# A two-layer decoder trunk on one core: every second weight block split into its two parts by GpSimd's transfers instead of by ScalarE and VectorE

## The chip, the cores and the metric

The kernel runs on one core of a Trainium2 chip. The metric is the device time of one execution in microseconds, as the median of the runs of a kernel; smaller is better. Beside it stands one execution taken by the hardware profiler, whose first to last instruction is the span.

## What is computed

The reference is a decoder trunk of two layers over 256 tokens with a model width of 2048, all in float32:

```
for i in range(2):
    hn = rms_norm(h, norm_mix[i])
    h = h + (sb_gla_mixer(hn, ...) if i == 0 else ssd_mixer(hn, ...))
    h = h + squared_relu_mlp(rms_norm(h, norm_mlp[i]), mlp_w_up[i], mlp_w_down[i])
    h = h + sigmoid(h @ ple_w_gate[i]) * (p[i] @ ple_w_proj[i])
return rms_norm(h, final_norm)
```

The first mixer is stick-breaking attention beside gated linear attention, the second a state-space mixer with a short convolution. Nearly all of the arithmetic lies in the dense products: the input projections of the mixers (2048 to some 6144 and 10240 columns), their output projections, the MLP (2048 to 8192 and back, twice) and the gate (2048 to 2048, twice). What matters here is that the weights, some 500 MB, are each used once, and that every product is to have nearly float32 accuracy.

## The kernel before, in words

Activations are held feature-major: a tile has 128 features on the partitions and the 256 tokens along the row. Each activation operand is kept as two parts side by side, a rounded part "hi" in the type float32r in columns 0 to 255 and the remainder "lo" in columns 256 to 511 (split_into, line 103). Weights are split in the same way. A product is then hi x hi + hi x lo + lo x hi.

feature_major (line 112) does almost all dense products. It takes groups of output columns (width 4 means four tiles of 128 columns, so four PSUM banks of 512 columns); for each group it goes over kb_n blocks of the contraction. A block is 1 MB: four 128-row slices of weights with 512 columns each, laid out as 128 partitions x 2048 elements. For every block it

- loads it into a tile wraw with one DMA on SP's queue (load_block, line 94; the very first block in two halves),
- and for each half block (two slices, 128 x 1024 elements, 512 KB) calls split_weights (line 85): ScalarE copies wraw into whi, rounding it (line 88), and VectorE writes wlo = wraw - whi (line 89),
- then issues, for each of the four banks, two matmuls with whi as the stationary operand against all 512 columns of the activation (hi and lo, line 128) and two with wlo against the 256 columns of the activation's hi (line 133).

So a half block is sixteen matmuls. After the last block of a group, evac is called for each bank: ScalarE copies the bank's right half out of PSUM (line 168), VectorE adds it to the left half (line 169), and what follows depends on the stage (a scaling at line 171; an addition into the residual on GpSimd at lines 274, 300 and 339; a split of the result into the next operand at lines 106 to 110). token_major (line 143) does the same for the value projections with the activation as the stationary operand; it covers 16 blocks of 1 MB.

The tiles wraw, whi and wlo come from one pool with three buffers each (line 55). A buffer is given to a new tile when all readers of the old one are done: a whi buffer when TensorE has run the half block's matmuls, a wraw buffer when VectorE has made both remainders. The order of the instructions on each engine's queue is fixed before the run by the tile framework, which plans it with the program's order as priority and inserts all waits; at run time every queue is in order. Small side computations of the mixers are woven between blocks by pace (line 401).

SP's queue carries the weight loads, ScalarE's queue some small loads and eight broadcasts. GpSimd issues no transfers; it does elementwise work of 0.7 to 1.2 us each, mostly the additions into the residual.

Of the kernel before, what the change touches and what calls it, by code (L numbers as in the profile page):

```python
# [16 lines left out]
P = 128  # L17
# [8 lines left out]
def hybrid_trunk(  # L26
# [56 lines left out]
    rstd2 = keep.tile([P, T], F32, name="rstd2")  # L83

    def split_weights(dst, src_raw, cols):
        hi = wts.tile([P, cols], F32R, tag="whi", name="whi", padded_shape=[P, 1024])
        lo = wts.tile([P, cols], F32R, tag="wlo", name="wlo", padded_shape=[P, 1024])
        nc.scalar.copy(out=hi, in_=src_raw)  # L88
        nc.vector.tensor_tensor(out=lo, in0=src_raw, in1=hi.bitcast(F32), op=ALU.subtract)  # L89
        return hi, lo  # L90

    halve = [True]

    def load_block(src, cols=2048):
        raw = wts.tile([P, cols], F32, tag="wraw", name="wraw", padded_shape=[P, 2048])
        if halve.pop() if halve else False:
            nc.sync.dma_start(raw[:, : cols // 2], src[:, : cols // 2])
            nc.sync.dma_start(raw[:, cols // 2 :], src[:, cols // 2 :])
        else:
            nc.sync.dma_start(raw, src)  # L100
        return raw
# [8 lines left out]
            nc.vector.scalar_tensor_tensor(out=lo, in0=value, scalar=g, in1=hi.bitcast(F32), op0=ALU.mult, op1=ALU.subtract)  # L110

    def feature_major(blocks, kb_n, xt, evac, width=4, kts=4, evac_last=None):
        """blocks: DRAM access patterns, kb_n per group of `width` output tiles."""
        for grp, srcs in enumerate(blocks):
            banks = [acc_ps.tile([P, 512], F32, tag="acc", name=f"acc{n}") for n in range(width)]
            cols = kts * width * P
            per = 1024 // (width * P)
            if per > kts:
                per = kts
            for kb in range(kb_n):  # L120
                raw = load_block(srcs[kb], cols)
                for c0 in range(0, kts, per):
                    hi, lo = split_weights(None, raw[:, c0 * width * P : (c0 + per) * width * P], per * width * P)
                    for n in range(width):
                        for j in range(per):
                            k = kb * kts + c0 + j
                            o = (j * width + n) * P
                            nc.tensor.matmul(banks[n], lhsT=hi[:, o : o + P], rhs=xt(k),  # L128
                                             start=(k == 0), stop=False, skip_group_check=True)
                        for j in range(per):  # L130
                            k = kb * kts + c0 + j
                            o = (j * width + n) * P
                            nc.tensor.matmul(banks[n][:, T : 2 * T], lhsT=lo[:, o : o + P], rhs=xt(k)[:, 0:T],  # L133
                                             start=False, stop=(k == kb_n * kts - 1), skip_group_check=True)
                yield
            if evac_last is not None and grp == len(blocks) - 1:
                evac_last(banks)
            else:
                for n in range(width):
                    evac(grp * width + n, banks[n])  # L140
            yield

    def token_major(blocks, kb_n, xt, evac):
        """out[token, column] with the activations stationary."""
        for grp, srcs in enumerate(blocks):
            banks = [acc_ps.tile([P, 512], F32, tag="acc", name=f"acct{n}") for n in range(2)]
            for kb in range(kb_n):
# [23 lines left out]
            nc.vector.tensor_tensor(out=dst, in0=dst, in1=scale, op=ALU.mult)  # L171

    def gate_silu(dst, half):
        """dst = silu(2 * half)."""
        th = ev.tile([P, T], F32, tag="s", name="th")
        nc.scalar.activation(th, half, AF.Tanh)
        nc.vector.scalar_tensor_tensor(out=dst, in0=th, scalar=1.0, in1=half, op0=ALU.add, op1=ALU.mult)
# [7 lines left out]
            (eng or nc.gpsimd).tensor_tensor(out=sq_acc, in0=sq_acc, in1=sq, op=ALU.add)  # L185

    def newton(r, v):
        """r = 1/sqrt(v), one step: r * (1.5 - 0.5 v r^2)."""
        nc.vector.tensor_tensor(out=v, in0=v, in1=r, op=ALU.mult)
        nc.vector.scalar_tensor_tensor(out=v, in0=v, scalar=-0.5, in1=r, op0=ALU.mult, op1=ALU.mult)  # L190
        nc.vector.scalar_tensor_tensor(out=r, in0=v, scalar=1.5, in1=r, op0=ALU.add, op1=ALU.mult)

    def rstd_steps(mean=mean_d, squared=False, extra=(), in_psum=False):
        """rstd[:, t] = 1/sqrt(mean over features of the squares of token t + EPS), on every partition."""
        ms = small_ps(2, "ms")
        parts = [sq_acc, *extra]
        for i, sq in enumerate(parts):
# [65 lines left out]
            pass  # L263

    def out_stage(w, kb_n, xt, which, scale=None, before=None):
        """h += scale * (x @ w); returns the next stage's operand, gain applied, not yet normalized."""
        nxt = new_x()

        def evac(n, bank):
# [47 lines left out]
        return nxt, px  # L317

    def ple(i, x, px, mid):
        """h += sigmoid(x @ w_gate) * pp; returns h with the next norm's gain (split, but after the last layer)."""  # L320
        last = i == 1
        extra = []
        pp = [page([P, 8, T], f"pp{m}") for m in range(2)]
# [66 lines left out]
        yield  # L390

    def staggered(gens):
        """Step generator i of `gens` at ticks i, i + 1, ...; one tick per step, the youngest first."""
        live, gens = [], list(gens)
        while gens or live:
            if gens:
# [2 lines left out]
            yield  # L399

    def pace(main, sides):
        """Trace main; a side [after, every, generator] takes a step at step `after` of main and each `every` steps later.

        Sides may be added while main is traced, with `after` None for the next step."""
        n = 0
        for _ in main:
            n += 1
# [563 lines left out]
```

## Time and profile before

| | |
|---|---|
| median of 2 runs | 2781.89 us (2781.86 to 2781.91) |
| profiled execution, span | 2781.0 us |
| TensorE matmul busy | 2741.3 us (99%) |
| VectorE, ScalarE, GpSimd busy | 1848.8 (66%), 1440.0 (52%), 445.0 us (16%) |
| moved by DMA | 508.85 MB, mean 183 GB/s |
| granted TensorE clock, mean | 0.995 |

How to read the lines: a group of instructions has its source line, engine, operation, output and inputs, shape and count, then busy time and the mean duration of one in ns, and after the bar the idle time of its engine just before these instructions, with what ended it. PE is TensorE, PEld its loading of stationary weights, DVE is VectorE, ACT is ScalarE, POOL is GpSimd, SPq the queue of SP. A row of a timeline has the start in us, the length, the instruction, and in brackets the idle time before it. A row of stretches has its limits, its length, the busy time of each engine with the number of instructions, then the granted TensorE clock, the busy share of the DMA engines and GB/s. A row of issues has the count, the KB of each transfer and the median time from issue to landing in us.

### The profile page before, as it was taken

Reading aid. Unit: us, or ns where it says so; the run is one execution under the profiler, and the core shown is the slowest. Engines: PE = TensorE matmul, PEld = TensorE weight load, DVE = VectorE, ACT = ScalarE, POOL = GpSimd, SP = SyncE. Lnnn points to the kernel's source line nnn. Section 1 sums busy time; section 2 is a strip of 40 time slices with the busy share of each in tenths; the row PEclk is TensorE's granted clock in tenths of the full one; section 3 lists DMA queues with packets and bytes.
Section 4 is the critical chain, followed back from the end, with each engine's and each line's share of the span. In section 5 each row is a group of like instructions: output and inputs, shape, how many; then the busy total and the mean of one; then the engine's idle time right before and its main releaser. Section 6 shows DMA issues by size and latency. Waiting matters only on the chain.

```text
span 2781.0 us, 40169 instructions
## 1 busy us (share of the span) xinstructions
PE 2741.3 (99%) x15724; PEld 2371.0 (85%) x15724; DVE 1848.8 (66%) x2692; ACT 1440.0 (52%) x2180; POOL 445.0 (16%) x510
## 2 busy tenths in 40 slices
PE   7999999999999999999999999999999999999998
PEld 6888888888888888888888888888888888888887
DVE  7455676665666666679987888765666566666665
ACT  6455455544444444466555565554544444454455
POOL 4000031002002022133132122321100201102212
PEclk9999999999999999999999999999999999999998
DMA  5544355555555555554555555455555555555553
GB/s 208 187 167 152 125 180 195 184 195 184 195 184 195 187 191 187 178 186 155 212 197 177 183 186 190 172 184 185 194 182 188 191 189 189 188 195 186 193 175 129
DMA packets 72672, 508.85 MB, mean 183 GB/s; under 512 B 8656, under 2 KB 8848, under 8 KB 11936
## 3 DMA queue, kind: packets, MB, share of 16 engines
q1 hardware_dynamic: 70416, 497.58, 51.5%
q10 hardware_dynamic: 2064, 8.69, 0.9%
q8 instruction: 123, 2.02, 0.3%
q14 instruction: 69, 0.57, 0.1%
HBM read 504.07 MB, written 2.16 MB: 182 GB/s over the span
## 4 chain that ended last, share of the span: by engine, by line
PE 93%; DVE 4%; ACT 1%; POOL 1%; issue 1%; DMA 1%; DVEq 0%; ACTq 0%; POOLq 0%
PE acc L128 58%; PE acc L133 29%; DVE wlo L89 1%; PE acct L158 1%; PE acct L159 1%; PE acct L157 1%; DVE x L110 1%; PE y_ps L554 1%; ACT whi L88 1%; DVE yx L110 0%; PE y_ps L556 0%; POOL hn L239 0%; PE gla_o L836 0%; PE xs_tp L530 0%; PE st_ps L545 0%
## 5 line engine op out<-in xcount | busy, mean ns | idle before, releaser
L89 DVE TENSOR_TENSOR wlo<-wraw,whi 128x1024 fp32r<-128x1024 f32 x940 | 1179.4, 1257 | 826.2 <-ACT whi L88 824.3
L88 ACT CAST whi<-wraw 128x1024 fp32r<-128x1024 f32 x940 | 986.6, 1051 | 1051.7 <-PE acc L128 988.0
L128 PE MATMUL acc<-x,whi 128*128 128x512 f32 x4384 | 1386.4, 398 | 14.1 <-ACT whi L88 8.6
L133 PEld LDWEIGHTS acc<-x,wlo 128*128 128x128 f32 x4384 | 820.8, 189 | 200.3 <-DVE wlo L89 9.8
L133 PE MATMUL acc<-x,wlo 128*128 128x256 f32 x4384 | 863.2, 279 | 4.6 <-DVE wlo L89 4.6
L128 PEld LDWEIGHTS acc<-x,whi 128*128 128x128 f32 x4384 | 674.2, 190 | 22.5 <-ACT whi L88 8.6
L128 PE MATMUL acc<-hid,whi 128*128 128x512 f32 x2048 | 643.5, 395 | 0.0
L133 PEld LDWEIGHTS acc<-hid,wlo 128*128 128x128 f32 x2048 | 384.8, 188 | 90.9
L133 PE MATMUL acc<-hid,wlo 128*128 128x256 f32 x2048 | 403.0, 278 | 0.0
L300 POOL TENSOR_TENSOR h<-h,t_dn 128x256 f32<-128x256 f32 x128 | 152.9, 1205 | 1267.7 <-DVE t_dn L171 1266.9
L128 PEld LDWEIGHTS acc<-hid,whi 128*128 128x128 f32 x2048 | 311.8, 189 | 0.0
L168 ACT COPY right<-acc 128x256 f32<-128x256 f32 x422 | 153.2, 367 | 67.5 <-PE acc L133 66.5
L128 PE MATMUL acc<-yx,whi 128*128 128x512 f32 x512 | 161.4, 396 | 1.2 <-DVE sz L608 1.2
L133 PEld LDWEIGHTS acc<-yx,wlo 128*128 128x128 f32 x512 | 96.1, 188 | 23.3 <-DVE wlo L89 0.7
L185 POOL TENSOR_TENSOR sq_acc<-sq_acc,sq 128x256 f32<-128x256 f32 x98 | 96.7, 987 | 47.6 <-ACT sq L184 45.7
L133 PE MATMUL acc<-yx,wlo 128*128 128x256 f32 x512 | 100.9, 278 | 0.3 <-DVE wlo L89 0.3
L274 POOL TENSOR_TENSOR h<-h,t_out 128x256 f32<-128x256 f32 x32 | 37.6, 1193 | 291.8 <-DVE t_out L169 154.5
L128 PEld LDWEIGHTS acc<-yx,whi 128*128 128x128 f32 x512 | 78.1, 189 | 1.4 <-DVE sz L608 1.4
L171 DVE TENSOR_TENSOR t_dn<-t_dn,rstd 128x256 f32<-128x256 f32 x128 | 72.0, 583 | 0.8
L484 DVE SCALAR_TENSOR_TENSOR a_cv<-xp,cw,a_cv 128x256 f32<-128x256 f32 x144 | 65.7, 486 | 0.2
L110 DVE SCALAR_TENSOR_TENSOR x<-h,gain,x 128x256 fp32r<-128x256 f32 x64 | 47.5, 769 | 19.6 <-ACT x L109 19.6
L107 DVE TENSOR_TENSOR hid<-s_up,hid 128x256 fp32r<-128x256 f32 x128 | 50.7, 417 | 0.5 <-ACT hid L106 0.5
(245 smaller groups left out, 1790.0 us busy)
## 6 DMA issues: line engine op xcount, KB each, us to landing
wraw<-in_mlp_up_dram SPq DMA_DIRECT2D x128, 1024.0 KB, 4.9
wraw<-in_mlp_down_dram SPq DMA_DIRECT2D x128, 1024.0 KB, 4.9
wraw<-in_ssd_in_dram SPq DMA_DIRECT2D x80, 1024.0 KB, 4.9
wraw<-in_ab_in_dram SPq DMA_DIRECT2D x47, 1024.0 KB, 4.9
wraw<-in_ple_gate_dram SPq DMA_DIRECT2D x32, 1024.0 KB, 4.9
wraw<-in_ssd_out_dram SPq DMA_DIRECT2D x32, 1024.0 KB, 4.9
wraw<-in_ab_out_dram SPq DMA_DIRECT2D x16, 1024.0 KB, 4.9
rb<-acs_rows ACTq DMA_DIRECT2D x8, 1024.0 KB, 4.7
```

Of the source, the lines that this page charges most:

```text
L88: nc.scalar.copy(out=hi, in_=src_raw)
L89: nc.vector.tensor_tensor(out=lo, in0=src_raw, in1=hi.bitcast(F32), op=ALU.subtract)
L107: nc.vector.tensor_tensor(out=lo, in0=value, in1=hi.bitcast(F32), op=ALU.subtract)
L110: nc.vector.scalar_tensor_tensor(out=lo, in0=value, scalar=g, in1=hi.bitcast(F32), op0=ALU.mult, op1=ALU.subtract)
L128: nc.tensor.matmul(banks[n], lhsT=hi[:, o : o + P], rhs=xt(k), start=(k == 0), stop=False, skip_group_check=True)
L133: nc.tensor.matmul(banks[n][:, T : 2 * T], lhsT=lo[:, o : o + P], rhs=xt(k)[:, 0:T], start=False, stop=(k == kb_n * kts - 1), skip_group_c ...
L168: nc.scalar.copy(out=right[:rows], in_=bank[:rows, T : 2 * T])
L171: nc.vector.tensor_tensor(out=dst, in0=dst, in1=scale, op=ALU.mult)
L185: (eng or nc.gpsimd).tensor_tensor(out=sq_acc, in0=sq_acc, in1=sq, op=ALU.add)
L274: nc.gpsimd.tensor_tensor(out=h[:, n, :], in0=h[:, n, :], in1=t, op=ALU.add)
L300: nc.gpsimd.tensor_tensor(out=h[:, n, :], in0=h[:, n, :], in1=t, op=ALU.add)
L484: nc.vector.scalar_tensor_tensor(out=a, in0=xp[:, i : T + i], scalar=cw[:, blk, i : i + 1], in1=a, op0=ALU.mult, op1=ALU.add)
```

## The change

In feature_major, with width 4 and kts 4, every block with odd kb is no longer loaded into wraw. For each of its halves a new function dma_split takes a whi and a wlo tile and issues three instructions: a transfer on GpSimd's queue from the weights in DRAM into whi, which converts from float32 to float32r; on ScalarE wlo = -1 x whi; and a second transfer on GpSimd's queue of the same weights that is added to what stands in wlo. Even blocks, token_major and the narrow products keep the load on SP's queue and split_weights. The buffers change: whi and wlo have four each instead of three, wraw two instead of three (4 KB and 8 KB per partition each, so the sum stays the same). The diff, without the removed docstrings:

```
     def split_weights(dst, src_raw, cols):
-        hi = wts.tile([P, cols], F32R, tag="whi", name="whi", padded_shape=[P, 1024])
-        lo = wts.tile([P, cols], F32R, tag="wlo", name="wlo", padded_shape=[P, 1024])
+        hi = wts.tile([P, cols], F32R, tag="whi", name="whi", padded_shape=[P, 1024], bufs=4)
+        lo = wts.tile([P, cols], F32R, tag="wlo", name="wlo", padded_shape=[P, 1024], bufs=4)
         nc.scalar.copy(out=hi, in_=src_raw)
         nc.vector.tensor_tensor(out=lo, in0=src_raw, in1=hi.bitcast(F32), op=ALU.subtract)
         return hi, lo
 
+    def dma_split(src, cols):
+
+        hi = wts.tile([P, cols], F32R, tag="whi", name="whi", padded_shape=[P, 1024], bufs=4)
+        lo = wts.tile([P, cols], F32R, tag="wlo", name="wlo", padded_shape=[P, 1024], bufs=4)
+        nc.gpsimd.dma_start(hi, src)
+        nc.scalar.mul(lo, hi.bitcast(F32), -1.0)
+        nc.gpsimd.dma_start(lo, src, accum_op=ALU.add)
+        return hi, lo
...
     def load_block(src, cols=2048):
-        raw = wts.tile([P, cols], F32, tag="wraw", name="wraw", padded_shape=[P, 2048])
+        raw = wts.tile([P, cols], F32, tag="wraw", name="wraw", padded_shape=[P, 2048], bufs=2)
...
             for kb in range(kb_n):
-                raw = load_block(srcs[kb], cols)
+                by_dma = width == 4 and kts == 4 and kb % 2 == 1
+                raw = None if by_dma else load_block(srcs[kb], cols)
                 for c0 in range(0, kts, per):
-                    hi, lo = split_weights(None, raw[:, c0 * width * P : (c0 + per) * width * P], per * width * P)
+                    cs = slice(c0 * width * P, (c0 + per) * width * P)
+                    if by_dma:
+                        hi, lo = dma_split(srcs[kb][:, cs], per * width * P)
+                    else:
+                        hi, lo = split_weights(None, raw[:, cs], per * width * P)
```

## The prediction

> **What bounds the kernel now.** I read the head of the page first, then its groups, then the table of waits of each engine, then the timeline of ScalarE in a stretch where nothing special happens, because the change acts on a steady rhythm and its price has to be a price per beat.
>
> ```profile
> span 2781.0 us, 40169 instructions
> PE 2741.3 (99%) x15724; PEld 2371.0 (85%) x15724; DVE 1848.8 (66%) x2692; ACT 1440.0 (52%) x2180; POOL 445.0 (16%) x510
> q1 hardware_dynamic: 70416, 497.58, 51.5%
> L89 DVE TENSOR_TENSOR wlo<-wraw,whi 128x1024 fp32r<-128x1024 f32 x940 | 1179.4, 1257 | 826.2 <-ACT whi L88 824.3
> L88 ACT CAST whi<-wraw 128x1024 fp32r<-128x1024 f32 x940 | 986.6, 1051 | 1051.7 <-PE acc L128 988.0
> ...
> wraw<-in_mlp_up_dram SPq DMA_DIRECT2D x128, 1024.0 KB, 4.9
> ```
>
> TensorE is busy 99% of the span: only 2781.0 - 2741.3 = 39.7 us (1.4%) are left to gain. The two engines that the change relieves are not what it waits for. ScalarE idles 1051.7 us before its casts, 988.0 of them until TensorE has let go of a weight buffer, and VectorE idles behind ScalarE. So the splitting keeps up and waits for buffers. The loads wait too (the row of q1: 51.5% of 16 engines' time for 497.58 MB).
>
> The rhythm, from ScalarE's timeline:
>
> ```profile
> 880.62 1.05 ACT L88 CAST whi<-wraw 128x1024 fp32r<-128x1024 f32 x1 [1.47 <-PE acc L128]
> 883.41 1.05 ACT L88 CAST whi<-wraw 128x1024 fp32r<-128x1024 f32 x1 [1.73 <-PE acc L128]
> 886.19 1.05 ACT L88 CAST whi<-wraw 128x1024 fp32r<-128x1024 f32 x1 [1.74 <-PE acc L128]
> 888.98 1.05 ACT L88 CAST whi<-wraw 128x1024 fp32r<-128x1024 f32 x1 [1.73 <-PE acc L128]
> 891.77 1.05 ACT L88 CAST whi<-wraw 128x1024 fp32r<-128x1024 f32 x1 [1.73 <-PE acc L128]
> ```
>
> Four casts take 891.77 - 880.62 = 11.15 us, so TensorE eats one half block (512 KB of weights) in T = 2.79 us and one pair of blocks (even and odd, four halves) in 11.15 us. Each cast starts when a buffer comes free and takes 1.05 us: the present lead is comfortable, since the split of a half takes 1.05 + 1.26 = 2.3 us against the two halves (5.6 us) that TensorE still has in store with three buffers.
>
> **How often the change applies.** Blocks of 1 MB with width 4 and kts 4 in feature_major: 128 (mlp_up) + 128 (mlp_down) + 80 (ssd_in) + 32 (ab_in, 8 of its 12 column groups) + 32 (ple_gate) + 32 (ssd_out) + 16 (ab_out) = 448. Every second is 224, so 224 pairs of 11.15 us = 2498 us of the span run in the new rhythm.
>
> **What is removed.** Of 940 casts 448 become a negation of the same 128x1024 on ScalarE: I price it at the cast's 1.05 us, so no change there. 448 subtractions leave VectorE: 448 x 1.257 = 563 us of busy time. That gains nothing, since VectorE idled 824.3 us for ScalarE already. 224 loads leave SP's queue; SP then loads only even blocks into two buffers, each free a whole pair before it is needed: 11 us against the 4.9 us of a load. Hidden; if that cover went, it would cost the difference, which is negative.
>
> **What is added, and where it lies.** Each of the 448 odd halves now needs: a DMA on GpSimd's queue into hi (it waits until TensorE has released that hi buffer), a negation on ScalarE (waits for the landing), a second DMA on GpSimd's queue that adds the weights into lo (waits for the negation), then TensorE (waits for the landing). Nothing in this chain can begin before a buffer is free. With four buffers and four halves per pair, an odd half gets the buffer of the odd half one pair earlier, so between that release and its own use TensorE has three halves to work on: the cover is 3 x 2.79 = 8.36 us. What the chain takes beyond that is a TensorE stall, once per pair: the second odd half begins its chain one T later and is needed one T later, so it comes just in time behind the first. Should GpSimd's order be hi, lo, hi, lo rather than hi, hi, lo, lo, the stall moves ahead of the second half, while the pair's period stays chain + T as long as twice (hi + negation) does not exceed it.
>
> No transfer by GpSimd's queue, no converting and no accumulating one is in this trace, so both are bounded by the nearest rows.
>
> The nearest rows to GpSimd's handling of an instruction, to a wait on ScalarE, and to SP's handling of a load:
>
> ```profile
> L300 POOL TENSOR_TENSOR h<-h,t_dn 128x256 f32<-128x256 f32 x128 | 152.9, 1205 | 1267.7 <-DVE t_dn L171 1266.9
> L168 ACT COPY right<-acc 128x256 f32<-128x256 f32 x422 | 153.2, 367 | 67.5 <-PE acc L133 66.5
> ```
> ```profile
> 878.50 2.47 POOL L300 TENSOR_TENSOR h<-h,t_dn 128x256 f32<-128x256 f32 x2 [16.47 <-DVE t_dn L171]
> 881.40 0.74 POOL L300 TENSOR_TENSOR h<-h,t_dn 128x256 f32<-128x256 f32 x1 [0.43 <-DVE t_dn L171]
> 882.56 1.59 POOL L300 TENSOR_TENSOR h<-h,t_dn 128x256 f32<-128x256 f32 x1 [0.43 <-DVE t_dn L171]
> ```
>
> ```profile
> 5.91 0.33 SPq L100 DMA_DIRECT2D wraw<-in_ab_in_dram  x1
> ```
>
> And to the transfers:
>
> ```profile
> wraw<-in_ple_proj_dram SPq DMA_DIRECT2D x8, 512.0 KB, 3.5
> h<-in_xT_dram SPq DMA_DIRECT2D x4, 512.0 KB, 7.7
> ```
> ```profile
> 0.00:20.00 20.00, 11.05 (x44) 8.73 (x45) 9.97 (x14) 13.46 (x28) 10.50 (x33) 1.00 0.84 318
> ```
>
> A transfer of 512 KB lands 3.5 us after issue when it has the engines nearly to itself and 7.7 us in the opening, where the engines are busy to 0.84 at 318 GB/s. 512 KB more costs 4.9 - 3.5 = 1.4 us.
>
> The hi transfer: 3.5 us at best, 7.7 at worst. I take 3.5 + 0.7 + 0.7 = 4.9. The first 0.7 is GpSimd's own handling, taken as the shorter of its elementwise instructions (0.74 us at 881.40), against 0.33 us on SP. The second is half of the 1.4 us by which SP's next 1 MB load would slow it when both run together: that load is issued when the second even half has been split, just about when the odd buffer comes free.
>
> The negation: 1.05 us, plus 0.2 of waiting behind half an evacuation copy (the row of L168): 1.25 us. Zero to 1.05 us more if it meets an even half's cast; I keep 1.25.
>
> The accumulating transfer: it must read what stands in lo besides the weights. At best the reading of lo is free, 3.5; at worst 7.7. I take 3.5 + 0.7 + 1.4 = 5.6: one more stream of 512 KB through the same engines, and GpSimd's handling.
>
> A page of notes speaks against the change here: the Trainium skill, "Collectives: The Full Stack", section "The bandwidth ceiling: the fold count and why AG ≠ RS ≠ AR", says that a reducing transfer needs two source reads on the same ring and so moves at about half a copy's rate. No run here shows it yet; with the extra stream as priced above the sum is the forecast, and with a free read the chain would be 1.4 us shorter per pair.
>
> Chain: 4.9 + 1.25 + 5.6 = 11.75 us. Stall: 11.75 - 8.36 = 3.39 us per pair, 224 x 3.39 = 759 us.
>
> **The stall's echo in the clock.** This trace shows what a gap of such a length does (first the stretches, then TensorE's timeline):
>
> ```profile
> 64.00:66.00 2.00, 0.00 (x0) 0.00 (x0) 1.56 (x3) 2.00 (x6) 0.00 (x0) 1.00 0.00 0
> 66.00:68.00 2.00, 1.32 (x4) 1.14 (x5) 2.00 (x7) 1.08 (x2) 0.00 (x0) 0.52 0.35 53
> 68.00:70.00 2.00, 2.00 (x9) 1.72 (x9) 2.00 (x4) 0.00 (x0) 0.00 (x0) 0.62 0.93 381
> ```
> ```profile
> 66.68 1.22 PE L128 MATMUL acc<-x,whi 128*128 128x512 f32 x2 [3.15 <-DVE q L169]
> 67.70 0.63 PE L133 MATMUL acc<-x,wlo 128*128 128x256 f32 x2
> 68.13 1.06 PE L128 MATMUL acc<-x,whi 128*128 128x512 f32 x2
> 68.98 0.63 PE L133 MATMUL acc<-x,wlo 128*128 128x256 f32 x2
> 69.41 0.68 PE L128 MATMUL acc<-x,whi 128*128 128x512 f32 x2
> ```
>
> After 3.15 us without a matmul the granted clock is 0.52, and the eight matmuls from 66.68 to 69.41 take 2.73 us. At the rhythm of T for sixteen they would take 1.39: a loss of 1.34 us. A gap of 3.39 us stands at that edge, so I charge half of the pairs: 224 x 0.67 = 150 us (zero to 300).
>
> **GpSimd's old work.** Its queue is in order, and it often waits at its head for an evacuation (1266.9 us in the row of L300). Four adds per group hold GpSimd from 878.50 to 884.15. A transfer queued behind all four goes out up to 5.65 us late. This can hit one pair of each group: 32 groups of mlp_down, 4 of ab_out, 4 of ssd_out and 8 of ple_gate, 48 x 5.65 = 271 us at most. I take zero, because the first odd transfer of a group is ready one T before the group ends and stands ahead if the queue is ordered by readiness, and keep 271 for the upper end.
>
> **Sum.** 2781.0 + 759 + 150 = 3690 us; the medians shown lie 0.9 us above the span (2781.89), so about 3690 stands, some 33% slower. A change of 2% (56 us) is about what a measurement can tell from none.
>
> **Rivals.**
>
> (a) Hidden, the other side. If both transfers land in the time of the 3.5 us row, the chain is 3.5 + 1.05 + 3.5 = 8.05 us, under the cover of 8.36: TensorE never waits and the time is 2781, or down to 2781 - 40 if the relieved VectorE also closes the few gaps. It decides at a landing of (8.36 - 1.05) / 2 = 3.65 us per transfer. For it: the row of 3.5. Against: that row is of a quiet stretch and another queue, and these transfers meet each other and SP's loads. The Trainium skill, "DMA: Bandwidth & Descriptors", section "Anatomy of one DMA — SWDGE (gpsimd) path", gives about 2.0 us plus bytes over 436e9 for a GpSimd transfer; by it 512 KB would take an estimated 3.2 us, and it is this rival. Chance 0.06 (0.01 of it faster by over 2%).
>
> (b) The engines' throughput decides, not latency. By q1's row 1.0486 MB costs 0.515 x 2781 x 1.0486 / 497.58 = 3.02 us of all 16 engines. A pair now takes 6.03 us of 11.15; with a plain load, a converting and an accumulating block at one and two streams 3.02 + 3.02 + 6.03 = 12.07. If the latency is hidden otherwise, the cost is 224 x 0.92 = 206 us: 2987 us. With a partly hidden chain this side covers 2840 to 3050. Chance 0.14.
>
> (c) Converting and accumulating run far below a copy. If each transfer takes 7.7 us the chain is 7.7 + 1.25 + 7.7 = 16.65, the stall 8.29; with a full 1.34 of clock 224 x 9.63 = 2157 us: 4938 us. For it: three streams share the engines. Against: the 7.7 is of an opening with the engines at 0.84, and the pair's 9.05 to 12.07 us of (b) would fill them to 0.61 to 0.82 of a period of 14.8. Chance 0.20.
>
> (d) The change does not do what it says (hi not rounded by the converting transfer, so lo is zero). Both transfers and the negation run whatever their values, so the time is that of the forecast; it takes no chance of its own.
>
> **How the numbers follow.** Forecast (stall of 1.2 to 6 us per pair, 3050 to 4130 with the clock): 0.60; (c) 0.20; (b) 0.14; (a) 0.06. The range reaches down to 2950, into (b) as far as its 2987, and up into (c) up to 4638, the 8.29 us of stall without the clock's loss: 2950 to 4640, which leaves out (a), half of (b) and the worst third of (c). Faster 0.01, same 0.05, slower 0.94.
>
> **What would show it.** The waits of TensorE name a DMA into wlo, about 224 times (or 448, if both halves stall) and 3 to 4 us each; busy TensorE falls to about 75 to 80% of the span and the granted clock falls in slices of the long stages. VectorE's busy time falls by about 560 us. The issue rows show 448 transfers each of 512 KB into whi and wlo, landing near 5 and near 5.6 us, the second longer than the first. Wrong, if TensorE stays near 99%; if its waits are for ScalarE's casts of even halves; if landings are 7 us or more; or if the DMA share is at 0.9 and more, which would make (b) or (c) the cause.

## The result, and the profile after

The changed kernel takes 3723.88 us (3722.17 to 3725.58) against 2781.89: the ratio is 1.339 (95% interval 1.336 to 1.341). The prediction was 3690, in a range of 2950 to 4640. The profiled execution has a span of 3720.5 us, 939.5 more than before.

The lines of the page after that answer to those of before:

```profile
span 3720.5 us, 40690 instructions
PE 3038.5 (82%) x15724; PEld 2537.4 (68%) x15724; DVE 1338.0 (36%) x2244; ACT 1429.5 (38%) x2180; POOL 985.1 (26%) x1406
...
q0 software_dynamic: 129024, 469.82, 58.1%
q1 hardware_dynamic: 38160, 262.69, 18.7%
...
L89 DVE TENSOR_TENSOR wlo<-wraw,whi 128x1024 fp32r<-128x1024 f32 x492 | 609.3, 1241 | 1478.2 <-ACT whi L88 1478.1
L97 ACT ACTIVATE wlo<-whi 128x1024 fp32r<-128x1024 f32 x448 | 474.6, 1060 | 1258.8 <-DMA whi<-in_mlp_down_dram 379.7
...
wraw<-in_mlp_up_dram SPq DMA_DIRECT2D x64, 1024.0 KB, 7.0
whi<-in_mlp_up_dram POOLq DMA_DIRECT2D x128, 512.0 KB, 4.4
wlo<-in_mlp_up_dram POOLq DMA_DIRECT2D x128, 512.0 KB, 5.6
```

TensorE does the same 15724 matmuls, but idles 3720.5 - 3038.5 = 682.0 us (39.7 before), and its busy time itself has grown by 297.2 us: 642 + 297 = 939. The mean granted clock is 0.923 instead of 0.995. VectorE's subtractions are down from 1179.4 to 609.3 us, which nobody needed. The new queue q0, on which GpSimd's transfers go, holds the DMA engines for 58.1% of the span; with all queues their share is 0.78.

What TensorE waits for is one thing; the first rows of its table of waits (us in total, times, longest):

```profile
PE acc L147 <- DMA wlo<-in_mlp_down_dram: 192.5, 72, 5.0
PE acc L147 <- DMA wlo<-in_mlp_up_dram: 187.1, 71, 4.9
```

With the five rows of the smaller stages these are 652 us in 251 waits, 2.6 us each: about one wait per pair. Only some 30 us of TensorE's idle time lie elsewhere. mlp_up and mlp_down have 64 pairs each and wait as long, though only mlp_down has the adds of L314 between its transfers.

One pair in order of time, from the timelines of GpSimd, ScalarE and TensorE (start, length, instruction, idle before it):

```profile
1211.28 0.56 POOL L96 DMA_DIRECT2D whi<-in_mlp_up_dram  x1 [5.47 <-PE acc L142]
1214.65 0.55 POOL L96 DMA_DIRECT2D whi<-in_mlp_up_dram  x1 [2.81 <-PE acc L147]
1217.13 0.89 POOL L98 DMA_DIRECT2D wlo<-in_mlp_up_dram  x1 [1.92 <-ACT wlo L97]
1219.99 0.88 POOL L98 DMA_DIRECT2D wlo<-in_mlp_up_dram  x1 [1.97 <-ACT wlo L97]
1225.55 0.56 POOL L96 DMA_DIRECT2D whi<-in_mlp_up_dram  x1 [4.68 <-PE acc L142]
```
```profile
1215.77 1.06 ACT L97 ACTIVATE wlo<-whi 128x1024 fp32r<-128x1024 f32 x1 [10.20 <-DMA whi<-in_mlp_up_dram]
```
```profile
1222.88 0.50 PE L147 MATMUL acc<-x,wlo 128*128 128x256 f32 x2 [2.26 <-DMA wlo<-in_mlp_up_dram]
```

Released and issued at 1211.28, hi has landed 4.49 us later (the negation starts at 1215.77); from there 1.36 us to the second issue, and 5.75 us to the matmul that reads lo. The chain is 1222.88 - 1211.28 = 11.60 us. TensorE had three halves (8.36 us) and the first bank's two hi matmuls (0.63 us) in store, and one bank of these ran at half clock, which adds some 0.4 us. So it worked until 1220.62, 9.34 us after the release, and then stood 2.26 us. The next chain begins at 1225.55, a period of 14.27 us against 11.15 before. Over the whole span it is 11.15 + 939.5 / 224 = 15.34 us per pair.

### The profile page after: what moved, and what is told of

It is laid out like the page before. It is cut to its first block, busy times and chain, and to the rows that moved or that the text cites. A ratio compares the mean times of both kernels' runs of the same rounds, so it can differ in the third digit from the quotient of the medians.

```text
span 3720.5 us, 40690 instructions
## 1 busy us (share of the span) xinstructions
PE 3038.5 (82%) x15724; PEld 2537.4 (68%) x15724; DVE 1338.0 (36%) x2244; ACT 1429.5 (38%) x2180; POOL 985.1 (26%) x1406
## 3 DMA queue, kind: packets, MB, share of 16 engines
q0 software_dynamic: 129024, 469.82, 58.1%
## 4 chain that ended last, share of the span: by engine, by line
issue 45%; DMA 18%; PE 16%; POOL 13%; DVE 4%; ACT 3%; POOLq 0%; DVEq 0%; ACTq 0%
PE acc L142 9%; DMA wlo<-in_mlp_down_dram 6%; POOL wlo L98 6%; PE acc L147 5%; POOL whi L96 4%; DMA wlo<-in_ssd_in_dram 3%; DMA whi<-in_ssd_in_dram 2%; DMA wlo<-in_mlp_up_dram 1%; DMA wlo<-in_ssd_out_dram 1%; DVE t_dn L185 1%; DMA wlo<-in_ab_out_dram 1%; DVE t_dn L183 1%; DMA wlo<-in_ple_gate_dram 1%; POOL sq_acc L199 1%; POOL h L314 1%
## 5 line engine op out<-in xcount | busy, mean ns | idle before, releaser
L142 PE MATMUL acc<-x,whi 128*128 128x512 f32 x4384 | 1477.1, 421 | 9.1 <-ACT whi L88 8.4
L147 PE MATMUL acc<-x,wlo 128*128 128x256 f32 x4384 | 939.0, 298 | 380.4 <-DMA wlo<-in_mlp_up_dram 187.1
L89 DVE TENSOR_TENSOR wlo<-wraw,whi 128x1024 fp32r<-128x1024 f32 x492 | 609.3, 1241 | 1478.2 <-ACT whi L88 1478.1
L97 ACT ACTIVATE wlo<-whi 128x1024 fp32r<-128x1024 f32 x448 | 474.6, 1060 | 1258.8 <-DMA whi<-in_mlp_down_dram 379.7
L147 PE MATMUL acc<-hid,wlo 128*128 128x256 f32 x2048 | 440.4, 299 | 192.7 <-DMA wlo<-in_mlp_down_dram 192.5
L88 ACT CAST whi<-wraw 128x1024 fp32r<-128x1024 f32 x492 | 509.7, 1040 | 129.9 <-PE acc L142 65.9
L96 POOL DMA_DIRECT2D whi<-in_mlp_up_dram x128 | 71.3, 557 | 497.0 <-PE acc L142 253.7
L96 POOL DMA_DIRECT2D whi<-in_mlp_down_dram x128 | 72.1, 563 | 457.6 <-PE acc L142 281.8
L98 POOL DMA_DIRECT2D wlo<-in_mlp_up_dram x128 | 113.3, 885 | 267.4 <-ACT wlo L97 162.9
L98 POOL DMA_DIRECT2D wlo<-in_mlp_down_dram x128 | 113.5, 886 | 211.7 <-ACT wlo L97 159.6
L314 POOL TENSOR_TENSOR h<-h,t_dn 128x256 f32<-128x256 f32 x128 | 97.6, 770 | 99.5 <-DVE t_dn L185 96.3
```

The costliest lines, as they stand in the source:

```text
L96: nc.gpsimd.dma_start(hi, src)
L97: nc.scalar.mul(lo, hi.bitcast(F32), -1.0)
L98: nc.gpsimd.dma_start(lo, src, accum_op=ALU.add)
L314: nc.gpsimd.tensor_tensor(out=h[:, n, :], in0=h[:, n, :], in1=t, op=ALU.add)
```

## The experiments

All runs change the changed kernel. "Per pair" is the time above the kernel before, divided by the 224 pairs (112 in the second run); the change has 4.2 us. The kernel before stood at 2780 to 2781 us beside all of them.

| run | us | ratio to before (95%) | per pair, us | TensorE idle | TensorE busy above 2741.3 |
|---|---|---|---|---|---|
| the change | 3723.9 | 1.336 to 1.341 | 4.2 | 682 | 297 |
| five whi buffers | 3546.2 | 1.272 to 1.277 | 3.4 | 559 | 246 |
| every fourth block | 3482.4 | 1.249 to 1.255 | 6.3 | 503 | 232 |
| second transfer plain | 3525.9 | 1.265 to 1.270 | 3.3 | 546 | 233 |
| added matmuls of zeros | 3845.1 | 1.378 to 1.387 | 4.8 | 502 | 589 with the added ones |
| converting transfer alone | 3087.0 | 1.107 to 1.113 | 1.4 | 223 | 125 |
| accumulating transfer alone | 3372.6 | 1.207 to 1.219 | 2.6 | 453 | 184 |
| five whi and wlo, loads in halves | 3674.5 | 1.316 to 1.326 | 4.0 | 638 | 299 |
| second half of every block | 4307.8 | 1.542 to 1.556 | 6.8 | 1045 | 528 |
| buffers alone | 2792.3 | 1.002 to 1.006 | 0.05 | 48 | 0 |
| no dependency | 3092.7 | 1.109 to 1.115 | 1.4 | 250 | 100 |
| even blocks not loaded | 3616.7 | 1.293 to 1.309 | 3.7 | 593 | 289 |
| both | 3086.1 | 1.106 to 1.113 | 1.4 | 244 | 95 |

### More lead for the first transfer

```
-        hi = wts.tile([P, cols], F32R, tag="whi", ..., bufs=4)
+        hi = wts.tile([P, cols], F32R, tag="whi", ..., bufs=5)
```

> The change with five whi buffers instead of four (wlo stays at four). Theory (latency): the changed kernel loses because hi transfer + negation + accumulating transfer, 11.6 us from 1211.28 to 1222.88 in its trace, outlast the three halves (8.4 us) and the first bank's hi matmuls (0.4 us) that TensorE has in store. One more whi buffer lets the hi transfer start one half (2.8 us) earlier, which covers nearly all of the stall: 2790 to 2950 us. Rival (throughput): the engines' shares of the changed kernel, 58.1% and 18.7% of 3720.5 us, are 9.7 + 2.8 (for the even block) = about 12.4 us per pair, more than TensorE's 11.15, so the time cannot fall below about 3065 us.

3546.2 us: the latency theory missed by some 600 us, and the rival's floor of 3065 was not reached either. 178 us came back, not 800. The earlier issue was mostly eaten by a later landing: the first transfer now takes 7.7 us instead of 4.4 (mlp_up). The rows of issues, then GpSimd's timeline and ScalarE's, then the engines' stretches of the same pair:

```profile
whi<-in_mlp_up_dram POOLq DMA_DIRECT2D x128, 512.0 KB, 7.7
```
```profile
1223.38 0.88 POOL L98 DMA_DIRECT2D wlo<-in_mlp_down_dram  x1 [5.49 <-ACT whi L88]
1223.93 0.89 POOL L96 DMA_DIRECT2D whi<-in_mlp_down_dram  x1
1226.36 0.56 POOL L96 DMA_DIRECT2D whi<-in_mlp_down_dram  x1 [1.54 <-PE acc L147]
```
```profile
1233.10 1.06 ACT L97 ACTIVATE wlo<-whi 128x1024 fp32r<-128x1024 f32 x1 [9.98 <-DMA whi<-in_mlp_down_dram]
```
```profile
1228.00:1230.00 2.00, 0.90 (x3) 0.90 (x4) 0.00 (x0) 0.00 (x0) 0.00 (x0) 0.74 1.05 383
1230.00:1232.00 2.00, 2.00 (x7) 1.61 (x7) 0.00 (x0) 0.00 (x0) 0.00 (x0) 0.50 1.03 391
```

The first transfer of the next pair, issued at 1223.93, goes out half a microsecond behind the second accumulating one of this pair, the next one follows at 1226.36, and the DMA engines are full (1.03 to 1.05 in the last column but one) until 1232. It has landed only when the negation starts at 1233.10, 9.2 us after its issue. A buffer more moved the issue, but much less the landing.

### Fewer pairs

```
-                by_dma = width == 4 and kts == 4 and kb % 2 == 1
+                by_dma = width == 4 and kts == 4 and kb % 4 == 3
```

> Only every fourth block (kb % 4 == 3) goes through GpSimd's transfers; buffers as in the change. Theory (latency): each of the 112 remaining pairs of odd halves still has only three halves of cover, so each costs the same 939 / 224 = 4.2 us: 2781 + 470 = about 3250 us. Rival (throughput): four blocks need 3 x 2.8 + 9.7 = 18 us of the engines against 22.3 us of TensorE, so there is room and the time falls to 2780 to 2850 us.

3482.4 us. The throughput rival falls: with half of the pairs and a DMA share near 0.6 the cost did not go away. But each pair costs 6.3 us, more than the 4.2 expected. One of them, from the timelines of GpSimd, ScalarE and TensorE:

```profile
1204.39 0.60 POOL L96 DMA_DIRECT2D whi<-in_mlp_down_dram  x1 [2.91 <-PE acc L147]
1211.84 0.89 POOL L98 DMA_DIRECT2D wlo<-in_mlp_down_dram  x1 [4.11 <-ACT wlo L97]
```
```profile
1210.48 1.06 ACT L97 ACTIVATE wlo<-whi 128x1024 fp32r<-128x1024 f32 x1 [8.33 <-DMA whi<-in_mlp_down_dram]
```
```profile
1217.33 0.67 PE L147 MATMUL acc<-hid,wlo 128*128 128x256 f32 x2 [4.42 <-DMA wlo<-in_mlp_down_dram]
```

The chain is 12.94 us here, 1.34 longer. hi's landing alone is 1.60 us longer (6.09 instead of 4.49 us), and the whole stall of 4.42 us is in one place. Over the span TensorE idles (503 - 40) / 112 = 4.1 us more per pair, where the change has 2.9, and its busy time grows by 232 / 112 = 2.1 us per pair, where the change has 1.3.

### The second transfer without accumulation

```
-        nc.gpsimd.dma_start(lo, src, accum_op=ALU.add)
+        nc.gpsimd.dma_start(lo, src)
```

> The second transfer overwrites lo instead of adding to it (the subtraction is left out of the result for odd blocks); all waits stay. Theory: it then lands like the first, 4.4 instead of 5.6 us after issue, so the stall shrinks by 1.2 us per pair, and part of the clock's loss with it: 3300 to 3470 us. Rival: reading the old lo costs nothing and the longer landing of the second transfer comes from its place in the queue: 3680 to 3740 us.

3525.9 us, 198 less, where 254 to 424 were expected. The second landing fell from 5.6 to 4.3 us as expected, but the first one grew from 4.4 to 5.0 us (mlp_up). So accumulation costs, but 745 us remain with two transfers in line that don't accumulate. The share of q0 gives the engines' price of a transfer:

```profile
q0 software_dynamic: 129024, 469.82, 44.8%
```

0.448 x 3519.8 / 896 = 1.76 us of all sixteen engines for 512 KB; in the change one pair of converting and accumulating transfers takes 0.581 x 3720.5 / 448 = 4.83 us, so accumulating takes 3.07, if converting costs as much as the plain second transfer.

### Work put into the gap

```
+                    if by_dma and c0 == 0:
+                        for i in range(8):
+                            nc.tensor.matmul(banks[i % width], lhsT=zero, rhs=xt(kb * kts), start=False, stop=False, ...)
```

> Eight matmuls with a stationary tile of zeros are added ahead of each odd block's first half (they add nothing to the sums), some 1.9 us of TensorE work placed where it would wait. Theory: the period is set by the chain, so the added work costs no time, the gap shrinks below 1 us and the granted clock returns to 0.99: the 297 us by which TensorE's busy time has grown go away, 3430 us. Rival 1: the slower clock is not made by the gaps: 3724 us. Rival 2: TensorE's own time sets the period: 3724 + 224 x 1.9 = 4150 us.

3845.1 us, which is none of the three. The added matmuls are busy some 450 us (277.5 + 127.6 + 31.9 in the three rows of the large stages, and the small ones). Less idle (682 to 502) and a smaller growth of the rest (297 to about 140) return some 338 us of that, and 112 us are left over between the two profiled spans (121 by the medians). The clock's mean went up from 0.923 to 0.970, so the gaps do make the slow clock. But the period did not get shorter with it: TensorE now stands twice in many pairs (349 waits for lo in 224 pairs), as in its timeline:

```profile
1312.69 0.50 PE L154 MATMUL acc<-hid,wlo 128*128 128x256 f32 x2 [1.92 <-DMA wlo<-in_mlp_down_dram]
1316.61 0.50 PE L154 MATMUL acc<-hid,wlo 128*128 128x256 f32 x2 [0.84 <-DMA wlo<-in_mlp_down_dram]
```

It seems that a slow first half had hidden that the second half's lo comes later than one T behind the first; no run shows this by itself. Also, the accumulating transfer lands a microsecond later (6.6 instead of 5.6 in mlp_up and mlp_down); why is open. In the pair shown SP's load of 1 MB was issued at 1311.11, while both accumulating transfers were under way; in the pair of the change shown above it came at 1222.29, just before the first one was read.

### Each transfer alone

Converting alone; SP loads the odd block as well, VectorE subtracts:

```
         nc.gpsimd.dma_start(hi, src)
-        nc.scalar.mul(lo, hi.bitcast(F32), -1.0)
-        nc.gpsimd.dma_start(lo, src, accum_op=ALU.add)
+        nc.vector.tensor_tensor(out=lo, in0=raw, in1=hi.bitcast(F32), op=ALU.subtract)
```

> The converting transfer alone: odd blocks are also loaded by SP, GpSimd's transfer makes hi, VectorE makes lo = wraw - hi as in the kernel before; no negation, no accumulating transfer; the bytes read from memory stay those of the change. Theory (the chain's length): hi landing 4.5 + subtraction 1.25 = 5.8 us, under the cover of 8.4: 2780 to 2830 us. Rival (reading each odd block twice, or GpSimd's queue as such, is what costs): over 3000 us.

Accumulating alone; SP loads the odd block as well, ScalarE casts it:

```
-        nc.gpsimd.dma_start(hi, src)
+        nc.scalar.copy(out=hi, in_=raw)
         nc.scalar.mul(lo, hi.bitcast(F32), -1.0)
         nc.gpsimd.dma_start(lo, src, accum_op=ALU.add)
```

> The accumulating transfer alone: odd blocks are also loaded by SP, ScalarE casts hi from the loaded block and writes lo = -hi, GpSimd's transfer adds the weights into lo. Theory (the chain's length): cast 1.05 + negation 1.05 + some 0.3 of waits + landing 5.6 = 8.0 us, just under the cover of 8.4 + 0.4: no stall from latency. By the engines' shares an accumulating 512 KB costs 3.06 us of all engines (4.82 per hi and lo in the change, less 1.76 per transfer without accumulation in the run with the plain second transfer), so a pair needs 2 x 2.8 + 2 x 3.06 = 11.7 us against TensorE's 11.15: 2850 to 3100 us. Rival (the accumulating transfer is latency only): 2780 to 2830 us.

3087.0 and 3372.6 us, both above what was expected. Both sums had used the landings of the change, about 4.5 and 5.6 us. They don't hold once SP's loads are back. The rows of issues of the converting run, then one of the accumulating run:

```profile
wraw<-in_mlp_up_dram SPq DMA_DIRECT2D x128, 1024.0 KB, 7.4
...
whi<-in_mlp_up_dram POOLq DMA_DIRECT2D x128, 512.0 KB, 7.2
```
```profile
wlo<-in_mlp_up_dram POOLq DMA_DIRECT2D x128, 512.0 KB, 6.9
```

With the subtraction behind it the converting chain is 7.2 + 1.25 = 8.45 us, which just uses up the cover of 8.4 to 8.8 (three halves and the first bank's hi matmuls), where a landing of 4.4 would have left 3 us to spare. The accumulating chain is a cast, a negation, some 0.3 us of waiting and the landing: 1.05 + 1.05 + 0.3 + 6.9 = 9.3 us and more. So with the accumulating transfer alone the kernel loses 591 us, with the converting one alone 305, where the change loses 942. These are not two shares of one sum, because both runs also have the loads of the odd blocks, which the change has not. In the converting run VectorE's subtractions of mlp_up and mlp_down wait as long for SP's loads (143.7 + 153.0 us) as for the converting transfer (164.6 + 113.1), so its 305 us are not the price of that transfer alone.

### More lead for both

All of whi and wlo get a fifth buffer, paid for by loading the even blocks in halves:

```
-        hi = ... bufs=4)   lo = ... bufs=4)
+        hi = ... bufs=5)   lo = ... bufs=5)
-        raw = wts.tile([P, cols], F32, tag="wraw", ..., padded_shape=[P, 2048], bufs=2)
+        raw = wts.tile([P, cols], F32, tag="wraw", ..., padded_shape=[P, 1024], bufs=3)
```

> The change with five whi and five wlo buffers; to make room, the even blocks are loaded by SP in halves of 512 KB into three buffers. Theory 1 (latency alone): cover 4 x 2.79 = 11.15 us against a chain of 11.6: below 2900 us. Theory 2, formed after the run with five whi buffers stayed at 3546: the transfers of a pair fill the engines for 12.4 us, so the floor is about 3065, and what lies above it is engine time lost while a queue stands at a wait: 3065 to 3450 us.

3674.5 us: 49 us back. The theory that more lead cures the stall missed once more, by over 770 us, and the second one, which counted the engines' time, by over 220. whi now lands 7.4 us after its issue and the loads of 512 KB 6.4 (mlp_up). Why this run is slower than the one with five whi alone, from which it differs by the fifth wlo buffer and the loads in halves, was not found.

### The second half of every block instead of every second block

```
-                by_dma = width == 4 and kts == 4 and kb % 2 == 1
+                    by_dma = mixed and c0 > 0
```

SP loads the first half of every block. Now one half in two goes by DMA, never two in a row.

> The same number of halves by GpSimd's transfers, but the second half of every block instead of both halves of every second block; SP loads the first halves (512 KB each). Buffers as in the change. Theory: in the change the two accumulating transfers of a pair follow each other, 3.06 us each on the engines against 2.79 us of TensorE, and the next pair's first transfer comes behind the second of them. Spread out, each chain meets only its own: two chains of 11.4 us per pair share a stall of 11.4 - 8.8 = 2.6 us: 3300 to 3450 us. Rival (only the bytes or only the chain count): 3680 to 3760 us.

4307.8 us, 584 more instead of some 350 less, the furthest from what was expected. GpSimd's timeline, then ScalarE's, TensorE's and the stretches:

```profile
1410.35 0.55 POOL L96 DMA_DIRECT2D whi<-in_mlp_up_dram  x1 [11.73 <-PE acc L143]
1410.88 0.93 POOL L98 DMA_DIRECT2D wlo<-in_mlp_up_dram  x1
```
```profile
1406.67 0.37 ACT L183 COPY right<-acc 128x256 f32<-128x256 f32 x1 [5.62 <-PE acc L148]
1407.95 0.37 ACT L183 COPY right<-acc 128x256 f32<-128x256 f32 x1 [0.91 <-PE acc L148]
1408.22 1.07 ACT L97 ACTIVATE wlo<-whi 128x1024 fp32r<-128x1024 f32 x1
```
```profile
1418.94 2.08 PE L148 MATMUL acc<-x,wlo 128*128 128x256 f32 x8 [3.70 <-DMA wlo<-in_mlp_up_dram]
```
```profile
1406.00:1408.00 2.00, 2.00 (x7) 1.81 (x8) 0.85 (x2) 0.42 (x2) 0.00 (x0) 0.50 0.06 16
1408.00:1410.00 2.00, 2.00 (x7) 1.61 (x7) 1.64 (x3) 1.85 (x4) 0.00 (x0) 0.50 0.00 0
...
1416.00:1418.00 2.00, 0.00 (x0) 0.00 (x0) 0.50 (x1) 1.06 (x1) 0.34 (x2) 0.87 1.08 221
```

Two queues hold this chain up. The negation starts at 1408.22, right behind two evacuation copies on ScalarE that wait for TensorE, though the DMA engines have been nearly idle (0.06) since 1406. It is done at 1409.29, but its accumulating transfer stands in GpSimd's queue behind the converting transfer of the next half, which waits until TensorE lets go of a buffer (11.73 us of idle). From 1408 to 1410 the DMA engines do nothing (0.00), then both transfers go out in one microsecond, the engines are full (1.08), and the lo lands 8.06 us after its issue instead of 5.6. With gaps of 3.7 (here) to over 5 us TensorE also runs at a clock of 0.50 much of the time. In the pair shown the order in the queues and the two landings at once set the chain, not the number of halves in store.

### The buffers alone

```
-                by_dma = width == 4 and kts == 4 and kb % 2 == 1
+                by_dma = width == 4 and kts == 4 and kb < 0
```

> The buffers of the change (whi and wlo four, wraw two) with no block going through GpSimd's transfers. Both theories: a load lands in 4.9 us and a wraw buffer is free 8.4 us before its next use, so nothing changes: 2775 to 2790 us. If it is slower, part of the 939 us belongs to the buffers and not to the transfers.

2792.3 us (ratio 1.002 to 1.006): two raw buffers instead of three and four split ones instead of three cost 11 us, a little more than expected and 1% of the change's cost.

### No dependency between the two transfers

The negation reads a constant tile of zeros, so it needs no landing. Everything else runs as before.

```
-        nc.scalar.mul(lo, hi.bitcast(F32), -1.0)
+        nc.scalar.mul(lo, zero[:, :cols].bitcast(F32), -1.0)
```

> All instructions of the change stay, but the negation reads a constant tile instead of hi, so the accumulating transfer no longer follows the converting one (the subtraction is left out of the result for odd blocks). Theory 1 (the chain's latency): from the buffer's release the two transfers now run side by side, 1.05 + 0.3 + 5.7 = about 7 us under a cover of 8.4 + 0.4: 2781 to 2850 us. Theory 2 (the engines' time): a pair still needs 2 x (1.76 + 3.06) + 2.8 = 12.4 us of all engines against 11.15 of TensorE: not below 3065 us, 3065 to 3250. What remains up to 3724 is then the price of the dependency.

3092.7 us. The order "hi lands, then the negation, then lo is issued" is worth 3723.9 - 3092.7 = 631 us, two thirds of the cost. The theory of latency alone had asked for 2850 at most; it had taken a landing of 5.7 us, but with both transfers of a half under way together they land 6.7 and 7.8 us after issue (mlp_up), so that 1.05 + 0.3 + 7.8 = 9.2 us stand against the cover of 8.8. The rest, 311 us, looked like the throughput of rival (b), as the second theory had it (3065 to 3250): the DMA share is 0.91. The next two runs take engine time away to try that.

### Even blocks not loaded, with and without the dependency

One block is loaded once into a tile "kept", and every even half is split from it (one raw buffer is left for the other stages), so 224 loads of 1 MB are gone, some 2.8 us of engines per pair:

```
-                raw = None if by_dma else load_block(srcs[kb], cols)
+                raw = kept[0] if mixed else load_block(srcs[kb], cols)
```

> The change, with every even block split from one tile that is loaded once (the loads of the even blocks and so their values are left out); odd blocks as in the change. Engine time per pair falls from 12.4 to 9.6 us, the chain of three steps stays. Theory 1 (the chain's latency alone): hi lands 4 instead of 4.5 us after issue at most, 3600 to 3720 us. Theory 2 (transfers stand in each other's way): SP's load no longer comes between, 3250 to 3550 us.

> Both together: the negation reads a constant tile and the even blocks are not loaded (both parts of the result are left out). Engine time per pair 9.6 us, no chain of transfers. Theory 2: with less engine time than TensorE's 11.15 us and no dependency nothing is left to wait for: 2781 to 2850 us. If it stays above 3000, GpSimd's own queue or its transfers' latency holds something that neither theory has.

With the dependency 3616.7 us: only 107 less, as the chain theory said (3600 to 3720) and not the throughput theory (3250 to 3550). Without it 3086.1: the same as with the loads, 3092.7, though the DMA share fell from 0.91 to 0.75; TensorE's waits for lo fell only from 216 to 198 us. So the 311 us are not the sum of the engines' time either; that expectation fell too. What they are is seen in one pair of the last run (GpSimd, TensorE, then the stretches):

```profile
912.25 0.55 POOL L96 DMA_DIRECT2D whi<-in_mlp_down_dram  x1 [6.95 <-PE acc L155]
913.57 0.86 POOL L98 DMA_DIRECT2D wlo<-in_mlp_down_dram  x1 [0.77 <-ACT right L190]
...
916.42 0.59 POOL L96 DMA_DIRECT2D whi<-in_mlp_down_dram  x1
...
918.42 0.89 POOL L98 DMA_DIRECT2D wlo<-in_mlp_down_dram  x1
```
```profile
925.86 0.51 PE L155 MATMUL acc<-hid,wlo 128*128 128x256 f32 x2 [1.35 <-DMA wlo<-in_mlp_down_dram]
```
```profile
910.00:912.00 2.00, 2.00 (x13) 1.74 (x12) 1.23 (x1) 0.25 (x1) 0.00 (x0) 1.00 0.13 25
912.00:914.00 2.00, 2.00 (x14) 1.73 (x13) 0.37 (x1) 1.69 (x3) 0.98 (x2) 1.00 0.25 51
914.00:916.00 2.00, 2.00 (x14) 1.73 (x13) 1.68 (x6) 1.37 (x3) 1.45 (x3) 1.00 0.93 227
```

The DMA engines are nearly idle (0.13, 0.25) until TensorE has released the pair's first buffer, and nearly full (0.93) from about 914 on. The four transfers of a pair are 2 x 4.83 = 9.7 us of engine time; behind an issue at 912.25 and some 1.7 us before the engines fill (from 912.25 to 914), the last of them would by this estimate be there at 912.25 + 1.7 + 9.7 = 923.65 at the earliest. It was read at 925.86, 7.44 us after its issue. TensorE had 4 x 2.79 = 11.15 us and the first bank's 0.46 to give, until 923.86. A share of 0.75 over the span is thus no slack: the burst has to fit between a release and a use. The missing 2 us of this pair are those by which the adds held the last issue (the negation ended at 916.34), but mlp_up, which has no adds, waits three quarters as long in total (43.6 us against 58.7 in mlp_down). This reading is argued from the stretches; no run that spreads the burst succeeded.

## Why the prediction was right, point by point

- **What is removed.** As predicted: VectorE's subtractions lost 570 us (563 predicted; its busy time as a whole fell by 511, not by about 560) and nothing came of it. SP's loads of the even blocks land later than priced (7.0 to 7.2 us, not 4.9), but TensorE hardly waits for ScalarE's casts of them (10.0 us, 8.4 of these in one wait at the start).
- **The chain.** 4.9 + 1.25 + 5.6 = 11.75 predicted; 4.49 + 1.36 + 5.75 = 11.60 in the pair shown. The parts were guessed in part from rows of other work: GpSimd's handling was taken from an elementwise add (0.74 us), where it issues a converting transfer in 0.56 us and an accumulating one in 0.89. The landings' medians, 4.2 to 4.9 and 5.5 to 5.7, put an end to rivals (a), which needed 3.65, and (c), which needed 7.7. The formula of the Trainium skill, "DMA: Bandwidth & Descriptors", section "Anatomy of one DMA — SWDGE (gpsimd) path", gave an estimated 3.2 us; the trace has 4.2 to 4.9, and the measurement decides.
- **The extra stream of the accumulating transfer.** Priced at 1.4 us of landing; the run without accumulation has 4.3 instead of 5.6, 1.3 us. Of the engines it takes 3.07 against 1.76 us, 1.74 times a converting transfer. What the Trainium skill, "Collectives: The Full Stack", section "The bandwidth ceiling: the fold count and why AG ≠ RS ≠ AR", says of the reducing step of a collective, about half a copy's rate because of two source reads, agrees roughly with this.
- **The stall.** 759 us predicted, 642 more idle measured; 3.39 us per pair predicted, 652 / 224 = 2.9 found (251 waits of 2.6 us in the mean where some 224 of 3 to 4 us were expected; TensorE busy 82%, not 75 to 80%). The cover was set at three halves, and the time that TensorE works on the first bank's hi before it needs lo was left out. By starts it is 0.46 us at full clock (1217.21 to 1217.67 in TensorE's timeline): 224 x 0.46 = 103 of the 117 us.
- **The clock.** 150 us predicted, 297 measured, the mis-sized term. The granted clock fell from 0.995 to 0.923, which is 0.077 x 3720.5 - 0.005 x 2781 = 273 us of it. A drop was priced at 1.34 us in half of the pairs; in the stretch shown at the end it costs 1.7, and 273 / 1.7 makes an estimated 160 drops, 7 for 10 pairs. The price rested on the first 2.73 us after a single gap. The two errors, 117 us too much and 147 too little, nearly cancel: 939 measured against 909. That the sum came so close is luck.
- **GpSimd's adds at zero.** They held: mlp_down (with adds) and mlp_up (without) wait 192.5 and 187.1 us.
- **Rival (b).** The engines' time over a whole pair did not set the time: in the change the DMA share is 0.78, and without the dependency the time is the same when the engines are eased by 2.8 us per pair (3086 and 3093).
- **Rival (c).** Its period of 14.8 us does not come out of the forecast's own sum (11.15 + 3.39 = 14.54, with the clock's 0.67 us 15.2). Its chance does not hang on it, and the landings decided.
- **The step that failed**, though the time did not show it: a landing was taken as a fixed latency and the cover as the number of halves in store. By that a fifth buffer should have ended the stall; it gave back 178 us, and 49 with both tiles deepened. Landings went from 4.4 to 7.7 us as soon as issues moved together, to 7.2 beside SP's loads, to 6.7 and 7.8 without the dependency, and one half per block, never two in a row, was the slowest of all. The forecast hit because it was summed for the very arrangement that ran.

Open: why lo lands a microsecond later in the run with added matmuls; why five and five is slower than five whi alone; and whether a spread burst would save the last 311 us. No version beat the kernel before, which had only 39.7 us of TensorE's idle time to lose.

## What to carry to other kernels

A transfer, a computation and a second transfer in line took their whole length here in every round of the buffer they share, 11.6 us, and what that exceeds the work that the bound engine has in store is paid every round. A landing is a price only for the arrangement it was measured in: add up the engine time of everything issued between a release and a use, and look at what stands ahead in an in-order queue. Relieving engines that already waited for the bound one bought nothing here.

## What the runs showed of the hardware

**Gaps of the same length drop the clock or do not.** A gap of 2.72 us was followed by half speed, one of 3.38 us two pairs later was not (TensorE, then the stretches):

```profile
1207.64 0.50 PE L147 MATMUL acc<-x,wlo 128*128 128x256 f32 x2 [2.72 <-DMA wlo<-in_mlp_up_dram]
1237.68 0.50 PE L147 MATMUL acc<-x,wlo 128*128 128x256 f32 x2 [3.38 <-DMA wlo<-in_mlp_up_dram]
```
```profile
1208.00:1210.00 2.00, 2.00 (x11) 1.72 (x10) 0.00 (x0) 0.00 (x0) 0.00 (x0) 0.68 0.96 190
1210.00:1212.00 2.00, 2.00 (x7) 1.67 (x7) 0.00 (x0) 0.00 (x0) 0.56 (x1) 0.50 0.89 365
...
1238.00:1240.00 2.00, 2.00 (x14) 1.74 (x13) 0.00 (x0) 0.00 (x0) 0.00 (x0) 1.00 1.07 223
```

So the forecast's "edge" near 3.39 us was read from one gap and is not sharp. The whole trace of the change has 221 gaps of 0.8 us and more before an lo matmul. A slow stretch follows none of the 21 below 1.75 us, 26 of the 72 from there to 2.5 us, 54 of the 72 from there to 3.5 us, and all 56 above. After the gap of 2.72 us the clock lost 2 x 0.32 + 2 x 0.50 = 1.64 us (1.7 with the start of the next stretch, at 0.97). That is half speed for about 3.4 us, the length of the window that the Trainium skill gives in "TensorE: Matmul & The Clock Gate", section "What's actually happening"; the "≥1 idle window" that it names before the drop is more than the 2.72 us seen here. In all runs but two, TensorE's busy time grew by 0.45 to 0.53 us for each us of added idle time; the converting run has 0.68, and the run with added matmuls can't be counted so.

**Transfers have a second price, in engine time.** For 512 KB all sixteen engines are held 1.40 us by a plain load from SP's queue (0.430 x 3088.3 over 497.58 MB in the converting run; 1.51 in the kernel before), 1.73 to 1.76 by GpSimd's converting or plain transfer and 3.04 to 3.07 by an accumulating one. These shares are not constants: the converting and the accumulating transfer of a half together took from 4.5 (no dependency) to 4.9 us (even blocks not loaded), 4.83 in the change.

**GpSimd's adds became faster.** In the change:

```profile
L314 POOL TENSOR_TENSOR h<-h,t_dn 128x256 f32<-128x256 f32 x128 | 97.6, 770 | 99.5 <-DVE t_dn L185 96.3
```

The same 128 adds took 1205 ns each before, and 1189 with the buffers alone. In the rows of before that the prediction shows, single adds take 0.74 us (881.40) or 1.59 (882.56). During the long one VectorE subtracts:

```profile
882.34 1.21 DVE L89 TENSOR_TENSOR wlo<-wraw,whi 128x1024 fp32r<-128x1024 f32 x1
```

In that trace the adds that stand alone in the timeline and meet no such subtraction all take 0.73 to 0.74 us, those that meet one 1.46 us in the mean. What counts is whether the two meet, not how many subtractions there are: the converting run has all 940 of them and 777 ns per add, the run with five whi and wlo buffers 492 and 1169 ns. The Trainium skill, "SBUF — State Buffer", section "Who interferes with whom", says that a VectorE instruction with two SBUF inputs contends with a GpSimd instruction that reads SBUF; the trace agrees.
